# A two-layer diffusion backbone on one core: layer 1's modulation as row sums on the Vector Engine, and an opening with fewer, larger loads and idle transposes

## The chip, the cores and the metric

The kernel runs on one core of one Trainium2 chip. The metric is the device time of one execution in microseconds (us), the median over runs. Engines are named as in the profile: PE (TensorE matmuls), PEld (its weight loads), DVE (VectorE), ACT (ScalarE), POOL (GpSimd) and SP (SyncE, which issues most loads). Each of them takes its own instructions in a fixed order.

## The reference

512 latent tokens and 256 context tokens of width 1024 pass through two layers. Each layer is a mixer and a SwiGLU, and each of these is led by a norm that a modulation vector shifts and scales, and closed by a gate from the same vector:

```python
silu_c = jax.nn.silu(c)
silu_cc = jax.nn.silu(c_ctx)
for layer in range(DEPTH):
    need_ctx = layer < DEPTH - 1
    mod = (silu_c @ w_mod[layer] + b_mod[layer])[:, None, :]
    modc = silu_cc @ w_mod[layer] + b_mod[layer]
    sh1, sc1, g1, sh2, sc2, g2 = jnp.split(mod, 6, axis=-1)
    csh1, csc1, cg1, csh2, csc2, cg2 = jnp.split(modc, 6, axis=-1)
    h = modulate(rms_norm(x, norm_mix[layer]), sh1, sc1)
    hc = modulate(rms_norm(ctx, norm_mix[layer]), csh1, csc1)
    ...
    x = x + g1 * y
    x = x + g2 * swiglu(modulate(rms_norm(x, norm_ffn[layer]), sh2, sc2), w_ffn_in[layer], w_ffn_out[layer])
    if need_ctx:
        ctx = ctx + cg1 * yc
        ...
return rms_norm(x, norm_out)
```

The modulation of a layer is thus a product of one vector of 1024 (`silu(c)`) with a matrix of 1024 x 6144, and of a second vector (`silu(c_ctx)`) with the same matrix. In layer 1 the context is used only through `csh1` and `csc1`, the first third; its gates and its SwiGLU are not needed. Layer 0's mixer is global and windowed attention; layer 1's is neighbourhood attention and an RWKV-7 scan in two directions, which the kernel does in chunks with a small inverse.

## The kernel before, in words

All is fp32. A big product is done as three matmuls of rounded numbers: a weight tile of 128x1024 is loaded (`fetch`, L133), ACT rounds it into a high part `whi` (L143), and the rest, the low part `wlo`, is a subtraction (L145) on DVE, or on POOL while the flag `lo_pool` is set. Activations are split alike (`hxh`, `hxl`), and `mm3` (L387 to L389) issues high by high, high by low and low by high. `early` makes such a weight ahead of its use, and `onto`, `ffn` and `proj_in` consume them. Two buffers of each part exist, so PE works on one weight while the next is made.

The program is one stream of Python generators: a main line (for example the SwiGLU of layer 0 for x) calls `step(rate)`, which moves side work (`aside`, `beside`) on by so many yields. A scheduling layer turns that into one order per engine. In the stage that matters here, the main line is layer 0's output projection and SwiGLU for x, and beside it run the chain of layer 1's context (`ctx_chain`, with the RWKV inputs, the inverse `rwkv_inverse`, L1255 to L1267, and the scan) and, at half its rate (`M0`), the last two thirds of layer 1's modulation, `mods(1, 1)` and `mods(1, 2)`.

`mods` (L198 to L245) handles 2048 outputs. For each group of them it loads weights on a queue (POOL's here; 16 loads of 512 KB for each third, two buffers) and issues 32 matmuls (L224) with `silu_c`, a 128x32 operand of which two columns are used, into one of four column strips of a PSUM tile (`ps_m` here). In layer 1's last two thirds a matmul has 256 columns, and each third is two such groups of 32 matmuls; elsewhere it has 128 columns, and a third is four groups. (The profile counts two records for each.) Then ACT copies the result (L234), PE transposes it (L238), and DVE adds the bias and writes `mod` (L242). What uses these values is the gate of layer 1's mixer and layer 1's SwiGLU, well after the stage, and the norm that leads layer 1 reads the first third, which `mods(1, 0)` has made earlier.

The opening is `start` (L736 on) with `even_in` (L446 on). SP loads x in eight pieces, two tables, the weights of layer 0's first third of the modulation in pieces of 512 KB into eight slots, and after every fourth one a weight of the input projection; after the first four, the context in four pieces. ACT squares x (L309), DVE adds the squares (L311), PE sums them over partitions (L319), DVE makes the reciprocal root (L106 to L113), PE spreads it (L339); PE does the modulation (L224, L238); DVE and ACT then make the normed activations (`norm_k`, L378 to L380: a product on DVE, the shift and rounding on ACT, the low part on DVE), and PE begins the first input block (L465 to L467). `start` yields between these pieces. In the whole opening `lo_pool` is set, so the low parts of the first weights are made on POOL.

Of the kernel before, what the change touches and what calls it, by code (L numbers as in the profile page):

```python
# [20 lines left out]
KD = 8  # L21
# [14 lines left out]

S0, S1, S2, S3 = 6, 8, 4, 6
# [32 lines left out]
class Net:  # L70
# [93 lines left out]
    def setup(self):  # L164
        nc, ctx = self.nc, self.ctx
        self.cp = self.pool(ctx, "consts")
        self.cc = self.const("cc", [P, KD, 2])
        self.ident = self.t(self.cp, [P, P], "ident")
        make_identity(nc, self.ident)
        self.ones = self.t(self.cp, [P, 1], "ones")  # L170
        nc.vector.memset(self.ones, 1.0)
        self.zero1 = self.t(self.cp, [P, 1], "zero1")
        nc.vector.memset(self.zero1, 0.0)
        self.sc = self.t(self.cp, [P, KD, 32], "silu_c")
        nc.vector.memset(self.sc, 0.0)
# [21 lines left out]
    def mods(self, l, g, tmp, raws, dma, tag="t", hold=False):  # L197
# [49 lines left out]
        yield  # L247

# [195 lines left out]
    def even_in(self, tmp, hx, hc, kst, vt, start, rest):  # L444
# [3 lines left out]
        for blk in range(3):  # L448
            accs = [self.bank() for _ in range(TTILES)]
            for kp in range(4):  # L450
                if kp == blk == 0:
                    next(start)
                wh, wl = self.weight(self.ins["w0in"][blk, kp], 1024)
# [284 lines left out]
    def start(self, tmp, raws, hs):  # L738
# [3 lines left out]
        (X, _), (C, _) = self.streams  # L742
        for k in range(KD):
            nc.sync.dma_start(X[:, k, :], self.ins["xt"][:, k, :])
        self.bmod, self.nrm = self.const("bmod", [P, 2, 48]), self.const("nrm", [P, 5, 8])
        n = 0

        def dma(dst, src):
            nonlocal n
            nc.sync.dma_start(dst, src)  # L750
            n += 1
            if n % 4 == 0:
                self.fetch(self.ins["w0in"][0, n // 4 - 1])
            if n == 4:
                for k in range(0, KD, 2):
                    nc.sync.dma_start(C[:, k : k + 2, :], self.ins["ct"][:, k : k + 2, :])
# [20 lines left out]
        self.lo_pool = True  # L777
        self.early(None)
# [3 lines left out]
        self.norm_gain(0, 0, slice(0, None, 4))  # L782
        norms(0, 0)
        for q in range(4):
            for i in range(12):
# [15 lines left out]
    def layer0(self):  # L801
        nc, V = self.nc, self.nc.vector
        with ExitStack() as c1:
# [8 lines left out]
            with ExitStack() as c2:  # L812
# [8 lines left out]
                start = self.start(tmp, [r[:, 2 * i : 2 * i + 2, :] for r in raws for i in range(4)], {0: hx, 1: hc})  # L821
# [85 lines left out]
            with ExitStack() as c2:  # L907
# [3 lines left out]
                with ExitStack() as c3:  # L911
                    np_ = self.pool(c3, "nm1", 2)
                    raws = [self.t(wm, [P, 1, 1024], "wmod", bufs=2) for _ in range(2)]
                    rest = itertools.chain(*[self.mods(1, g, wm, raws, nc.gpsimd.dma_start, "m", True) for g in (1, 2)])
# [768 lines left out]
    def run(self):  # L1683
        self.setup()
        self.load_x()
        self.dr = self.pool(self.ctx, "dram", 1, bass.MemoryType.DRAM)
        self.biasd = self.t(self.dr, [P, 8, 4, 256], "biasd")
        self.layer0()
        self.layer1()


def prep(inputs):
# [9 lines left out]
    d["cc"] = c_(np.stack([g["c"][0], g["c_ctx"]], 1).reshape(KD, P, 2).transpose(1, 0, 2))  # L1702
    for l in range(2):
        for h in range(3):
            n = P if (l, h) < (1, 1) else 2 * P
            w = g["w_mod"][l][:, 2048 * h : 2048 * h + 2048].reshape(KD, P, 4, 512 // n, n).transpose(3, 1, 0, 2, 4)
            d[f"wmod{l}{h}"] = c_(w.reshape(512 // n, P, KD, 4 * n))
    d["bmod"] = c_(g["b_mod"].reshape(2, 48, P).transpose(2, 0, 1))
    nr = np.stack([g["norm_mix"][0], g["norm_ffn"][0], g["norm_mix"][1], g["norm_ffn"][1], g["norm_out"]])
    d["nrm"] = c_(nr.reshape(5, KD, P).transpose(2, 0, 1))  # L1710
# [80 lines left out]
```

## Time and profile before

| | |
|---|---|
| median of 3 runs | 2091.7 us (2090.3 to 2098.65) |
| the profiled execution | 2095.34 us, span 2093.4 us |
| mean granted TensorE clock | 0.967 |
| PE busy | 1981.8 us, 95% of the span |
| DVE busy | 1229.4 us, 59% |
| ACT busy | 893.1 us, 43% |
| POOL busy | 247.4 us, 12% |
| HBM traffic | 129 GB/s over the span |

A group's row of the profile reads: line, engine, operation, output<-inputs by the program's names, tile shape, count, busy time, mean ns of one, then the idle time of the engine just before and what ended it. A timeline's row starts with the start and the length of a run of equal instructions. In a table of stretches the granted clock (1.00 is full speed) stands behind the engines. Lines are those of the kernel before.

### The profile page before, as it was taken

The page shows a single profiled execution, that of the slowest core. Times are in us where ns is not written, and L with a number is a line of the kernel's source. Part 1 is how long each engine was busy: PE and PEld are TensorE (multiplying, and loading weights), DVE is VectorE, ACT ScalarE, POOL GpSimd, SP SyncE. Part 2 cuts the span into 40 slices and gives each one's busy share as a digit, 9 for nine tenths or more (in the row PEclk, how much of TensorE's full clock was granted, in tenths as well). Part 3 has the DMA queues.
Part 4 walks back from the last instruction along what each step waited for, and adds up shares of the span by engine and source line. Part 5 has one row for each costly group of instructions (what it writes and reads, how often), then busy time and mean ns, then how long its engine had stood idle before and what let it go on. Part 6 is the DMA issues. An engine that isn't in the chain of part 4 may idle for free.

```text
span 2093.4 us, 38293 instructions
## 1 busy us (share of the span) xinstructions
PE 1981.8 (95%) x15556; PEld 1611.0 (77%) x15556; DVE 1229.4 (59%) x2407; ACT 893.1 (43%) x1682; POOL 247.4 (12%) x366
## 2 busy tenths in 40 slices
PE   6999999999988999999999999889899989999997
PEld 4766778999986888787777776667667768888887
DVE  5756676666666443559445655775766774333335
ACT  3335557775733433552222355535345443222222
POOL 1111100000000010000112132322322120000000
PEclk9999999999999999999999998988889999999999
DMA  7353322444484445433434323455675133232321
GB/s 272 124 200 122 142 91 81 142 126 127 135 271 160 151 156 151 140 108 107 146 102 132 111 71 92 123 158 161 162 222 144 33 121 101 92 101 91 101 92 49
DMA packets 112655, 272.66 MB, mean 130 GB/s; under 512 B 15424, under 2 KB 48736, under 8 KB 110944
## 3 DMA queue, kind: packets, MB, share of 16 engines
q1 hardware_dynamic: 100256, 224.74, 34.4%
q0 software_dynamic: 12224, 45.49, 6.6%
q8 instruction: 122, 2.00, 0.4%
q14 instruction: 53, 0.43, 0.1%
HBM read 238.20 MB, written 31.98 MB: 129 GB/s over the span
## 4 chain that ended last, share of the span: by engine, by line
PE 74%; DVE 11%; issue 9%; DMA 2%; ACT 2%; POOL 1%; SPq 0%; DVEq 0%; POOLq 0%; ACTq 0%
PE ps_b L387 16%; PE ps_b L389 16%; PE ps_b L388 16%; PE ps_v L637 4%; PE ps_a L587 2%; PE ps_e L609 2%; PE ps_w L1311 2%; PE ps_w L1317 2%; PE ps_s L1340 1%; DVE kb L1262 1%; PE ps_w L1330 1%; DVE kb L1255 1%; DVE pi L1259 1%; PE ps_a L1047 1%; PE ps_e L1218 1%
## 5 line engine op out<-in xcount | busy, mean ns | idle before, releaser
L143 ACT CAST whi<-wraw 128x1024 fp32r<-128x1024 f32 (+2 forms) x291 | 292.7, 1008 | 669.8 <-PE ps_b L388 509.4
L145 DVE TENSOR_TENSOR wlo<-wraw,whi 128x1024 fp32r<-128x1024 f32 (+2 forms) x251 | 296.1, 1180 | 213.5 <-ACT whi L143 207.5
L387 PE MATMUL ps_b<-hxh,whi 128*128 128x512 f32 (+1 forms) x1040 | 402.4, 390 | 13.0 <-ACT cj L978 7.2
L388 PE MATMUL ps_b<-hxl,whi 128*128 128x512 f32 (+1 forms) x1040 | 397.8, 385 | 1.6 <-DVE hxl L380 1.5
L389 PE MATMUL ps_b<-hxh,wlo 128*128 128x512 f32 (+1 forms) x1040 | 397.3, 384 | 0.3 <-DVE wlo L145 0.2
L387 PEld LDWEIGHTS ps_b<-hxh,whi 128*128 128x128 f32 x1040 | 198.6, 192 | 60.6 <-ACT cj L978 7.8
L388 PEld LDWEIGHTS ps_b<-hxl,whi 128*128 128x128 f32 x1040 | 199.0, 192 | 40.1 <-DVE hxl L380 3.0
L389 PEld LDWEIGHTS ps_b<-hxh,wlo 128*128 128x128 f32 x1040 | 198.7, 192 | 39.6 <-DVE wlo L145 1.3
L387 PE MATMUL ps_b<-act,whi 128*128 128x512 f32 (+1 forms) x570 | 200.5, 352 | 4.6 <-ACT whi L143 2.8
L389 PE MATMUL ps_b<-act,wlo 128*128 128x512 f32 (+1 forms) x570 | 197.0, 346 | 1.5 <-DVE wlo L145 1.5
L388 PE MATMUL ps_b<-act,whi 128*128 128x512 f32 (+1 forms) x570 | 196.7, 345 | 0.6 <-DVE act L124 0.6
L387 PE MATMUL ps_b<-hch,whi 128*128 128x256 f32 x552 | 159.6, 289 | 0.1
L389 PE MATMUL ps_b<-hch,wlo 128*128 128x256 f32 x552 | 156.2, 284 | 0.4 <-DVE wlo L145 0.4
L388 PE MATMUL ps_b<-hcl,whi 128*128 128x256 f32 x552 | 155.9, 283 | 0.0
L387 PEld LDWEIGHTS ps_b<-act,whi 128*128 128x128 f32 x570 | 109.5, 192 | 22.7 <-issue 5.5
L389 PEld LDWEIGHTS ps_b<-act,wlo 128*128 128x128 f32 x570 | 109.6, 192 | 15.0 <-DVE wlo L145 2.1
L388 PEld LDWEIGHTS ps_b<-act,whi 128*128 128x128 f32 x570 | 109.6, 192 | 12.9 <-DVE act L124 1.0
L420 DVE SCALAR_TENSOR_TENSOR xx<-ps_b,mod,xx 128x512 f32<-128x512 f32 (+1 forms) x64 | 43.7, 684 | 120.6 <-PE ps_b L389 119.3
L145 POOL TENSOR_TENSOR wlo<-wraw,whi 128x1024 fp32r<-128x1024 f32 (+1 forms) x40 | 88.5, 2217 | 204.6 <-ACT whi L143 180.0
L713 DVE TENSOR_TENSOR ff_a<-ff_a,ps_b 128x512 f32<-128x512 f32 x44 | 30.2, 687 | 134.3 <-PE ps_b L389 133.6
L387 PEld LDWEIGHTS ps_b<-hch,whi 128*128 128x128 f32 x552 | 104.7, 190 | 5.7 <-issue 2.5
L389 PEld LDWEIGHTS ps_b<-hch,wlo 128*128 128x128 f32 x552 | 104.4, 190 | 1.7 <-DVE wlo L145 1.4
(373 smaller groups left out, 3470.6 us busy)
## 6 DMA issues: line engine op xcount, KB each, us to landing
wraw<-in_ffi SPq DMA_DIRECT2D x132, 512.0 KB, 3.5
xx<-in_wmod POOLq DMA_DIRECT2D x48, 512.0 KB, 5.0
wraw<-in_w1in SPq DMA_DIRECT2D x43, 512.0 KB, 3.6
wraw<-in_ffo SPq DMA_DIRECT2D x48, 448.0 KB, 3.3
wmod<-in_wmod POOLq DMA_DIRECT2D x32, 512.0 KB, 4.8
wraw<-in_ffo SPq DMA_DIRECT2D x24, 512.0 KB, 3.5
op<-op SPq DMA_DIRECT2D x32, 384.0 KB, 4.2
qx<-in_wmod SPq DMA_DIRECT2D x16, 512.0 KB, 6.7
```

The costliest lines, as they stand in the source:

```text
L143: self.nc.scalar.copy(hi[:, 0:n], raw)
L145: e.tensor_tensor(lo[:, 0:n], raw, hi[:, 0:n].bitcast(F32), op=ALU.subtract)
L387: mm(out, lhsT=wh, rhs=hh, start=first, stop=False)
L388: mm(out, lhsT=wh, rhs=hl, start=False, stop=False)
L389: mm(out, lhsT=wl, rhs=hh, start=False, stop=last)
L420: self.nc.vector.scalar_tensor_tensor(X[:, m, c], ps[:, 0:n][:, c], gate[:, m, i : i + 1], X[:, m, c], op0=ALU.mult, op1=ALU.add)
L587: nc.tensor.matmul(o, lhsT=q, rhs=k[:, b : b + o.shape[1]], start=i == 0, stop=i == len(passes) - 1)
L609: nc.tensor.transpose(pt[:, P * (j - c) : P * (j - c) + P], p[:, P * j : P * j + P], self.ident)
L637: self.nc.tensor.matmul(ps[HD * u : HD * u + HD, col : col + P], lhsT=vs[u][j], rhs=pts[u][:, j, :], start=j == 0, stop=j == nk - 1, tile_ ...
L713: V.tensor_tensor(a, a, pg[1][:, 0:w], op=ALU.mult)
L1311: mm(wy[HD * u + HD - W_ + r : HD * u + HD, p, :], lhsT=G[top[u], p, r:W_], rhs=VU[top[u], p, u, :], start=p == 0, stop=False, skip_group_ ...
L1317: mm(o, lhsT=AR[:, p, :], rhs=Sd[:, p, u, :], start=False, stop=not lat, skip_group_check=True)
```

## The change

There are four edits. First, the last two thirds of layer 1's modulation are made another way. The matrix is given transposed, so that 128 outputs lie on 128 partitions and the 1024 inputs along the row. The vector silu(c) is spread over all partitions by eight transposes and two ACT copies, and each of 32 tiles of 128 outputs is one DVE instruction, `tensor_tensor_reduce`, which multiplies the row by the vector, sums it and starts from the bias. Each is kept in its program order against all of DVE's other work. There are still 32 loads of 512 KB on POOL's queue, in three buffers; the next load is issued after each reduction. The second vector's values for these two thirds, which nothing uses, are set to zero. The 128 matmuls, their transposes, copies and bias additions are gone.

Second, the opening's loads: x as two pieces of 1 MB at the head of SP's queue, one table instead of three, the modulation's weights in pieces of 1 MB into four slots, a projection weight after every second, and the context as one piece after the third.

Third, 60 transposes of the identity into a PSUM bank that is overwritten later, issued in the program at the first input block.

Fourth, the first `early` comes after `norm_gain`, and `lo_pool` is set only after the first round, so that two low parts are made on DVE instead of POOL.

```diff
+    def mod_rows(self, l, tiles, tmp, dma, tag):
+        nc, V = self.nc, self.nc.vector
+        s = self.t(tmp, [P, 1024], "silu_r", bufs=1)
+        for h in range(2):
+            ps = self.bank(tag)
+            for j in range(4):
+                self.spread(ps[:, P * j : P * j + P], self.sc[:, 4 * h + j, 0:1].broadcast_to([P, P]))
+            nc.scalar.copy(s[:, 512 * h : 512 * h + 512], ps)
+        V.memset(self.mod[l][:, tiles[0] : tiles[-1] + 1, 1], 0.0)
+        todo, ahead = iter(tiles), []
+        def load():
+            t = next(todo, None)
+            if t is not None:
+                ahead.append(self.t(tmp, [P, 1024], "wmod", bufs=3))
+                dma(ahead[-1], self.ins[f"wmodT{l}"][t - tiles[0]])
+        load(), load(), load()
+        yield
+        for t in tiles:
+            w = ahead.pop(0)
+            self.tc.keep_in_program_order(
+                V.tensor_tensor_reduce(w, w, s, 1.0, self.bmod[:, l, t : t + 1], ALU.mult, ALU.add, self.mod[l][:, t, 0:1])
+            )
+            load()
+            yield
...
                 if kp == blk == 0:
                     next(start)
+                    for _ in range(WARM):
+                        nc.tensor.transpose(accs[0][:, 0:P], self.ident, self.ident)
...
-        for k in range(KD):
-            nc.sync.dma_start(X[:, k, :], self.ins["xt"][:, k, :])
-        self.bmod, self.nrm = self.const("bmod", [P, 2, 48]), self.const("nrm", [P, 5, 8])
...
-            if n % 4 == 0:
-                self.fetch(self.ins["w0in"][0, n // 4 - 1])
-            if n == 4:
-                for k in range(0, KD, 2):
-                    nc.sync.dma_start(C[:, k : k + 2, :], self.ins["ct"][:, k : k + 2, :])
+            if n % 2 == 0:
+                self.fetch(self.ins["w0in"][0, n // 2 - 1])
+            if n == 3:
+                nc.sync.dma_start(C, self.ins["ct"])
...
-        self.lo_pool = True
-        self.early(None)
...
         self.norm_gain(0, 0, slice(0, None, 4))
+        self.early(None)
         norms(0, 0)
         for q in range(4):
+            self.lo_pool = q > 0
...
-                    raws = [self.t(wm, [P, 1, 1024], "wmod", bufs=2) for _ in range(2)]
-                    rest = itertools.chain(*[self.mods(1, g, wm, raws, nc.gpsimd.dma_start, "m", True) for g in (1, 2)])
+                    rest = self.mod_rows(1, range(16, 48), wm, nc.gpsimd.dma_start, "m")
```

The order of the engines shows where this lands. The lines of the changed kernel are some 7 to 36 higher than those of the one before (the modulation's matmul L224 is L231 there, its transpose L238 is L245, the input block's L465 to L467 are L503 to L505, the spread L339 is L375, `mm3` L387 to L389 is L423 to L425, the low part L145 is L146, the inverse's L1259 and L1262 are L1292 and L1295).

First, PE at the start of the program, before; `qx` holds modulation weights, `hxh` and `hxl` the normed activations, `ps_t` and `ps_b` are PSUM tiles:

```order
L319 MATMUL ps_t_200<-ones_65,qc_136 128x1 x4
L224 MATMUL ps_t_219<-qx_45_130,silu_c_69 32x128 x8
L339 MATMUL ps_t_263<-ident_60,rms0y_206 128x128 x3
L224 MATMUL ps_t_219<-qx_45_130,silu_c_69 32x128 x8
L339 MATMUL ps_t_263<-ident_60,rms0y_206 128x128
L224 MATMUL ps_t_219<-qx_45_130,silu_c_69 32x128 x16
L238 MATMUL ps_t_269<-ident_60,qc_136 128x128
L465 MATMUL ps_b_179<-whi_259,hxh_11_85 128x512
```

And the same place in the changed kernel, where L490 is the idle transpose:

```order
L490 MATMUL ps_b_162<-ident_67 128x128 x29
L355 MATMUL ps_t_183<-ones_72,qc_138 128x1 x4
L231 MATMUL ps_t_202<-qx_45_132,silu_c_76 32x128 x16
L490 MATMUL ps_b_162<-ident_67 128x128 x8
L375 MATMUL ps_t_240<-ident_67,rms0y_189 128x128 x4
L231 MATMUL ps_t_202<-qx_45_132,silu_c_76 32x128 x16
L490 MATMUL ps_b_162<-ident_67 128x128 x4
L245 MATMUL ps_t_246<-ident_67,qc_138 128x128
L490 MATMUL ps_b_162<-ident_67 128x128 x19
L503 MATMUL ps_b_162<-whi_251,hxh_11_87 128x512
```

The 60 transposes stand in four places: ahead of everything, after the first half of the modulation's matmuls, before the transpose of their result, and before the first matmul of the input block.

Second, PE where layer 0's SwiGLU is led by its norm, before; `ps_m` is the modulation of layer 1, `rms0y` and `rms1y` are reciprocal roots:

```order
L339 MATMUL ps_b_7689<-ident_60,rms1y_7124 128x128 x2
L224 MATMUL ps_m_8140<-wmod_7245,silu_c_69 32x256 x4
L224 MATMUL ps_m_8140<-wmod_7246,silu_c_69 32x256 x4
L339 MATMUL ps_e_7756<-ident_60,rms0y_7610 128x128 x2
L319 MATMUL ps_e_7759<-ones_65,sq_a_1553_7273 128x1 x2
L224 MATMUL ps_m_8140<-wmod_7245,silu_c_69 32x256 x4
L224 MATMUL ps_m_8140<-wmod_7246,silu_c_69 32x256 x4
L387 MATMUL ps_b_7754<-hxh_1643_7726,whi_7744 128x256
```

And in the changed kernel:

```order
L375 MATMUL ps_b_7726<-ident_67,rms1y_7163 128x128 x2
L375 MATMUL ps_m_8031<-ident_67,silu_c_76 128x128 x4
L375 MATMUL ps_e_7793<-ident_67,rms0y_7647 128x128 x2
L355 MATMUL ps_e_7796<-ones_72,sq_a_1549_7310 128x1 x2
L375 MATMUL ps_m_8037<-ident_67,silu_c_76 128x128 x4
L423 MATMUL ps_b_7791<-hxh_1639_7763,whi_7781 128x256
```

Where the first sixteen modulation matmuls stood among the norm's spreads, the eight transposes of silu(c) stand now.

Third, DVE inside the inverse of layer 1's context (its steps are L1259 and L1262; `wlo` is the low part of a weight), before:

```order
L145 TENSOR_TENSOR wlo_10273<-wraw_10270,whi_10272 128x1024
L1259 TENSOR_TENSOR pi_10251<-kb_10249,kb_10250 128x87
L1262 TENSOR_TENSOR kb_10250<-kb_10250,pi_10251 128x29x3
L1259 TENSOR_TENSOR pi_10251<-kb_10249,kb_10250 128x112
L1262 TENSOR_TENSOR kb_10250<-kb_10250,pi_10251 128x28x4
L1259 TENSOR_TENSOR pi_10251<-kb_10249,kb_10250 128x135
```

And in the changed kernel, where L280 is the reduction and, as a row of its own, the read of its accumulator:

```order
L146 TENSOR_TENSOR wlo_10324<-wraw_10321,whi_10323 128x1024
L125 TENSOR_TENSOR act_10265<-ff_a_2066_10263,act_10264 128x512
L1292 TENSOR_TENSOR pi_10272<-kb_10270,kb_10271 128x156
L1295 TENSOR_TENSOR kb_10271<-kb_10271,pi_10272 128x26x6
L280 ISA wmod_9985,mod_9_80<-wmod_9985,silu_r_8030,c_tab_65 128x1024
L280 ISA mod_9_80 128x1
L1292 TENSOR_TENSOR pi_10272<-kb_10270,kb_10271 128x175
L1295 TENSOR_TENSOR kb_10271<-kb_10271,pi_10272 128x25x7
```

Eight of the 32 reductions stand between the first and the last step of that inverse; 15 stand ahead of it and nine behind it.

More of the change, by code (lines that the diff above doesn't have):

```diff
@@ L35 @@
 NKB = 2
+WARM = 60
 S0, S1, S2, S3 = 6, 8, 4, 6
@@ L165, in setup @@
         nc, ctx = self.nc, self.ctx
+        self.load_x()
+        X = self.streams[0][0]
+        for k in range(0, KD, 4):
+            nc.sync.dma_start(X[:, k : k + 4, :], self.ins["xt"][:, k : k + 4, :])
         self.cp = self.pool(ctx, "consts")
-        self.cc = self.const("cc", [P, KD, 2])
+        tab = self.const("tab", [P, 152])
+        self.cc = tab[:, 0:16].rearrange("p (k s) -> p k s", s=2)
+        self.bmod, self.nrm = (tab[:, a:b].rearrange("p (l j) -> p l j", l=l) for a, b, l in ((16, 112, 2), (112, 152, 5)))
         self.ident = self.t(self.cp, [P, P], "ident")
@@ L741, in start @@
         nc = self.nc
-        (X, _), (C, _) = self.streams
-        for k in range(KD):
-            nc.sync.dma_start(X[:, k, :], self.ins["xt"][:, k, :])
-        self.bmod, self.nrm = self.const("bmod", [P, 2, 48]), self.const("nrm", [P, 5, 8])
+        C = self.streams[1][0]
         n = 0
@@ L820, in layer0 @@
                 tmp = Slots(self.t(ap_, [P, 16 * NCTX], "qc"), 2)
-                start = self.start(tmp, [r[:, 2 * i : 2 * i + 2, :] for r in raws for i in range(4)], {0: hx, 1: hc})
+                start = self.start(tmp, [r[:, 4 * i : 4 * i + 4, :] for r in raws for i in range(2)], {0: hx, 1: hc})
                 next(start)
@@ L1684, in run @@
         self.setup()
-        self.load_x()
         self.dr = self.pool(self.ctx, "dram", 1, bass.MemoryType.DRAM)
@@ L1701, in prep @@
     d["ct"] = c_(g["ctx"][0].T.reshape(KD, P, NCTX).transpose(1, 0, 2))
-    d["cc"] = c_(np.stack([g["c"][0], g["c_ctx"]], 1).reshape(KD, P, 2).transpose(1, 0, 2))
+    cc = np.stack([g["c"][0], g["c_ctx"]], 1).reshape(KD, P, 2).transpose(1, 0, 2)
     for l in range(2):
         for h in range(3):
[L1705 to L1708, printed above, removed]
+            if (l, h) < (1, 1):
+                w = g["w_mod"][l][:, 2048 * h : 2048 * h + 2048].reshape(KD, P, 4, 4, P).transpose(3, 1, 0, 2, 4)
+                d[f"wmod{l}{h}"] = c_(w.reshape(4, P, KD, 4 * P))
+    d["wmodT1"] = c_(g["w_mod"][1][:, 2048:].T.reshape(32, P, KD * P))
+    bmod = g["b_mod"].reshape(2, 48, P).transpose(2, 0, 1)
     nr = np.stack([g["norm_mix"][0], g["norm_ffn"][0], g["norm_mix"][1], g["norm_ffn"][1], g["norm_out"]])
-    d["nrm"] = c_(nr.reshape(5, KD, P).transpose(2, 0, 1))
+    nr = nr.reshape(5, KD, P).transpose(2, 0, 1)
+    d["tab"] = c_(np.concatenate([x.reshape(P, -1) for x in (cc, bmod, nr)], 1))
     w = g["w_in_even"][0]
```

## The prediction

> **What bounds the kernel now.** I read the page first: the shares of the engines and the chain that ended last.
>
> ```profile
> span 2093.4 us, 38293 instructions
> PE 1981.8 (95%) x15556; PEld 1611.0 (77%) x15556; DVE 1229.4 (59%) x2407; ACT 893.1 (43%) x1682; POOL 247.4 (12%) x366
> PE 74%; DVE 11%; issue 9%; DMA 2%; ACT 2%; POOL 1%; SPq 0%; DVEq 0%; POOLq 0%; ACTq 0%
> ```
>
> TensorE is busy for 95% of the span and is 74% of the chain. So an instruction taken from PE is worth its own time, but only in stages where PE is what ends last; DVE holds 11% of the chain, so there are stages where work given to DVE costs as much. The stages decide. The next view is the table of stretches over all engines, from the end of layer 0's mixer to layer 1's opening, where all of the removed matmuls stand. Columns: stretch, its length, then busy time (with instructions) of PE, PEld, DVE, ACT and POOL, granted clock, DMA share, GB/s.
>
> ```profile
> 650.00:665.00 15.00, 9.10 (x79) 6.21 (x77) 13.43 (x43) 7.26 (x15) 2.10 (x4) 0.80 0.59 187
> 665.00:690.00 25.00, 24.63 (x180) 18.95 (x181) 16.06 (x42) 10.88 (x22) 3.16 (x6) 0.91 0.49 157
> 690.00:930.00 240.00, 238.45 (x1478) 196.47 (x1477) 108.08 (x158) 107.87 (x177) 11.18 (x35) 1.00 0.46 140
> 930.00:1000.00 70.00, 67.24 (x340) 53.35 (x339) 59.20 (x97) 17.32 (x21) 0.00 (x0) 0.98 0.38 119
> 1000.00:1170.00 170.00, 170.00 (x1579) 128.29 (x1578) 79.02 (x125) 46.30 (x74) 28.88 (x49) 1.00 0.39 123
> 1170.00:1190.00 20.00, 16.41 (x149) 13.89 (x149) 11.88 (x29) 6.08 (x12) 4.82 (x4) 0.78 0.41 147
> 1190.00:1210.00 20.00, 16.73 (x116) 14.04 (x115) 16.72 (x46) 9.33 (x18) 3.62 (x4) 0.93 0.07 26
> ```
>
> In 665 to 930 and 1000 to 1170 PE has no room and DVE is under half busy, save at the start. In 650 to 665 and 930 to 1000 it is the other way: DVE 13.43 of 15 and 59.20 of 70.
>
> **What the removed matmuls cost.** The same stretches for the modulation's PSUM tile alone (its matmuls and transposes):
>
> ```profile
> 650.00:665.00 15.00, 3.23 (x32) 0.82 (x32) 0.00 (x0) 0.00 (x0) 0.80 0.59 187
> 665.00:690.00 25.00, 6.73 (x50) 1.75 (x50) 0.24 (x2) 0.37 (x1) 0.91 0.49 157
> 690.00:930.00 240.00, 7.12 (x76) 2.44 (x76) 0.24 (x2) 0.38 (x1) 1.00 0.46 140
> 930.00:1000.00 70.00, 0.00 (x0) 0.00 (x0) 0.00 (x0) 0.00 (x0) 0.98 0.38 119
> 1000.00:1170.00 170.00, 8.77 (x88) 2.75 (x88) 0.31 (x2) 0.37 (x1) 1.00 0.39 123
> 1170.00:1190.00 20.00, 2.22 (x17) 0.78 (x17) 0.00 (x0) 0.37 (x1) 0.78 0.41 147
> sum 560.00, PE 28.67 PEld 8.72 DVE 1.01 ACT 1.49; mean PE 4.10 PEld 1.25 DVE 0.14 ACT 0.21
> PE ps_m L224 <- DMA wmod<-in_wmod: 6.0, 4, 2.7
> ```
>
> So 28.67 us of PE go. The last row is from the waits of PE in 600 to 1200: four times PE, which takes its queue in order, stood 6.0 us in all before a modulation matmul whose weights had not landed. In 650 to 665 that and the 3.23 us are mostly cover for the norms on DVE (13.43 of 15), so I count 0.8 us there. In 665 to 690 PE is full and the 6.73 us count: together 7.5. In 690 to 930 the 7.12 count, in 1000 to 1170 the 8.77. The rest (28.67 less the rows above, 2.8 us) lies in 1170 to 1210, where PE idles 6.9 us in 40 and the norms of layer 1 set part of the pace: I count 2.0. Sum: 7.5 + 7.1 + 8.8 + 2.0 = 25.4 us gained. Added to PE there: eight transposes that spread silu(c), about 1 us with their place in the queue. The 32 loads stay on the POOL queue with their size; the four ACT copies become two.
>
> **What the reductions cost.** 32 of them go to DVE, each over 128x1024 with two SBUF operands and a read of the accumulator. The trace shows no such one. The nearest rows: a custom DVE operation of 512 columns with its accumulator read, and ordinary subtractions of 512 and 1024 columns from two SBUF operands.
>
> ```profile
> L598 DVE CUSTOM_DVE_ANT_0 sm_p<-ps_a,zero,sm_m 128x512 f32<-128x512 f32 x32 | 23.9, 746 | 4.3 <-PE ps_a L587 3.9 <-ACT sm_p L599 0.2
> L598 DVE DVE_READ_ACCUMULATOR2_ANT sm_m<- 128x1 f32 x64 | 5.3, 83 | 0.0
> L145 DVE TENSOR_TENSOR wlo<-wraw,whi 128x512 fp32r<-128x512 f32 x8 | 5.5, 683 | 0.0
> L145 DVE TENSOR_TENSOR wlo<-wraw,whi 128x1024 fp32r<-128x1024 f32 x195 | 238.4, 1223 | 189.1 <-ACT whi L143 183.6
> ```
>
> 512 more columns cost 1223 - 683 = 540 ns, so a reduction is estimated at 746 + 540 + 83 = 1.37 us, 32 of them 44 us. The upper bound is two passes of 746 for each half and twice that rate: 2 x 746 x 2 less overheads, some 2.5 us. I take 1.37, because the 1223 ns row already has two SBUF operands and falls on the line of its smaller form.
>
> [...]
>
> Where do they lie? DVE takes its queue in order and each reduction is held at its place in the program, so what stands behind one is late by its length: most often the next low part of a weight (L145), and behind that PE. By the order, eight reductions stand inside the decoding of layer 1's inverse, the one place where DVE has no room:
>
> ```profile
> 935.71 8.37 DVE L1255 STREAM_TRANSPOSE kb<-G 32x1024 f32<-32x1024 f32 x4 [0.23 <-PE ps_e L1220]
> 935.00:950.00 15.00, 15.00 (x69) 12.29 (x69) 14.14 (x23) 3.37 (x4) 0.00 (x0) 1.00 0.37 106
> 950.00:965.00 15.00, 14.75 (x65) 11.50 (x64) 14.42 (x30) 5.25 (x7) 0.00 (x0) 1.00 0.26 73
> 965.00:980.00 15.00, 13.20 (x50) 10.11 (x49) 14.21 (x32) 2.50 (x3) 0.00 (x0) 0.89 0.26 85
> ```
>
> No modulation matmul stood there, so PE gains nothing, and 8 x 1.37 = 11 us of DVE are added to a stretch in which DVE idles 2.2 us in 45. The low parts between the steps of the inverse feed PE, so PE waits about what is left: 9 us lost (between 3, if the two weights that are ready ahead absorb it, and 18, at 2.4 us each). Outside, a low part waits on ACT's cast before it for 183.6 us in all, so a reduction mostly falls into that wait; with a few where the weight's matmuls are short, I take 1.5 us lost (0 to 5).
>
> **The opening.** PE's timeline and two neighbours of it, before:
>
> ```profile
> 12.17 1.87 PE L319 MATMUL ps_t<-ones,qc 128*128 128x1 f32 x8 [12.17 <-DVE qc L311]
> 18.58 1.94 PE L224 MATMUL ps_t<-qx,silu_c 128*32 128x128 f32 x32
> 20.91 0.33 PE L238 MATMUL ps_t<-ident,qc 128*128 128x128 f32 x1 [0.39 <-ACT qc L234]
> 23.32 0.73 PE L465 MATMUL ps_b<-whi,hxh 128*128 128x512 f32 x2 [2.08 <-ACT hxh L379]
> 24.78 1.22 PE L466 MATMUL ps_b<-wlo,hxh 128*128 128x512 f32 x2 [0.73 <-POOL wlo L145]
> 31.39 0.39 PE L467 MATMUL ps_b<-whi,hxl 128*128 128x512 f32 x1
> 35.23 1.95 PE L224 MATMUL ps_t<-qx,silu_c 128*32 128x128 f32 x64
> 42.28 0.50 PE L465 MATMUL ps_b<-whi,hxh 128*128 128x512 f32 x1 [2.00 <-ACT hxh L379]
> 24.00:31.00 7.00, 6.27 (x15) 4.45 (x15) 5.57 (x10) 3.72 (x9) 0.73 (x1) 0.51 1.04 405
> 38.55 2.38 POOL L145 TENSOR_TENSOR wlo<-wraw,whi 128x1024 fp32r<-128x1024 f32 x1 [13.82 <-ACT whi L143]
> 38.63 2.84 DVE L378 SCALAR_TENSOR_TENSOR qc<-xx,an,qc 128x512 f32<-128x512 f32 x1
> L378 DVE SCALAR_TENSOR_TENSOR qc<-xx,an,qc x8: 739/750/2899, 21.8 to 63.1; 128x512 f32<-128x512 f32 x8
> ```
>
> Three things can be won. First, a cold PE: 32 records take 1.94 us at 18.58 and 64 take 1.95 at 35.23, and in 24 to 31 the granted clock is 0.51. In 7 us that is 3.4 us of matmul time, and about 2 us more on the way to 23.32. The 60 idle transposes are to keep PE running ahead of it; 19 of them stand between L238 and the first L465, where PE waits 2.08 us. Second, the low part on POOL: L466 waits for it 0.73 us, and the norm on DVE at 38.63 takes 2.84 us beside it where its shortest is 0.739; so the wait of 2.00 us at 42.28 should go with the second low part moved to DVE, at the price of 1.2 us twice on DVE. Third, fewer and larger loads: the first square can start only when 1 MB of x has landed instead of 256 KB, the last one is about as early, so I count half a microsecond lost there and half gained by the shorter queue of issues. These overlap, since DVE is itself busy 5.57 of 7 us in 24 to 31: of 3.4 + 2 + 2 = 7.4 us I take 4.5 (0 to 7.4).
>
> [...]
>
> **The sum.** Against the profiled execution's 2095.3 us (its span is 2093.4): -4.5 (opening) - 25.4 (matmuls) + 1 (spread) + 9 (inverse) + 1.5 (late low parts) = -18.4 us, hence 2076.9 for such an execution. The median of the runs, 2091.7, lies 3.6 below this execution; I apply the same difference to it: 2073. About 0.5%, 10.5 us, is what a measurement here can tell from no change; faster thus means below 2081.3.
>
> **The rivals.**
> Forecast, all terms about as above: 2073, chance 0.50.
> Full gain: the weights ready ahead cover the reductions in the inverse (3 us instead of 9, nothing elsewhere) and the opening gives 7. That is 2073 - 6 - 1.5 - 2.5 = 2063. For it: at 935.71 DVE spends 8.37 us on transposes and PE stays at 15.00 of 15. Against: PE falls to 13.20 of 15 by 965. Chance 0.15.
> [...] Chance 0.12.
> [...] Chance 0.16.
> Slower: the reductions wait for their loads. Each load is issued by POOL only after the reduction that frees its buffer, and POOL's queue also holds steps of layer 1's scan over the context (28.88 us busy in 1000 to 1170); a load behind such a step is late, the reduction held in its place waits for it, and DVE, the low parts behind it and PE with them. By the order nine reductions stand in that stage. At 3.2 us late each on PE it is 29 us: 2073 + 29 = 2102, the point from which the change loses by 0.5%. For it: PE stood 6.0 us before such loads already. Against: three buffers instead of two, and 170 us for nine reductions, some 19 us from one to the next. Chance 0.07.
>
> **How the numbers follow.** Faster: forecast, full gain and no warming, 0.77, less 0.02 for the far end of the inverse's price: 0.75. Same: half rate and that far end, 0.18. Slower: 0.07. The range leaves out the slow case and a part beyond the full gain: from 2058 (the full gain and the parts of 25.4 that I did not count, 3.3 us, and 2 us on the low parts' path) to 2088 (half rate, with 3.5 us less won in the opening).
>
> **What would show it.** Right: the stretch after 650 shows no modulation matmul, each reduction takes 1.3 to 1.5 us, PE is still full in the stretches of 690 to 930 and 1000 to 1170, which are shorter by 7 and 9 us, PE's idle time in the inverse grows by about 9, and layer 0's second weight starts near 38 instead of 42.28. Wrong: reductions above 2 us; waits of DVE's reductions for their loads; a granted clock of half after the first input matmul; or PE's idle time in the inverse unchanged, which would put the gain near 2063.

## The result, and the profile after

The changed kernel takes 2080.55 us (median of 5 runs, 2078.02 to 2084.48), the one before 2096.36 us beside it (5 runs, 2090.3 to 2098.65). The ratio is 0.9935, with a 95% interval from 0.9913 to 0.9957: 13.6 us faster by that ratio (15.8 by the two medians), where the sum gave 18.4. The change profiled at 2083.11 us, 12.2 less than the execution before. In what follows two executions are left out because they fell in a slow state: 2214.03 us in double_rows, which is the profiled one, so that kernel has no profile to compare by stages, and 8934.53 us in double_others. The page after, at its head:

```profile
span 2081.3 us, 37907 instructions
PE 1970.1 (95%) x15360; PEld 1615.4 (78%) x15360; DVE 1263.2 (61%) x2466; ACT 893.9 (43%) x1681; POOL 246.9 (12%) x364
PE 74%; DVE 12%; issue 6%; DMA 3%; ACT 2%; POOL 1%; SPq 0%; DVEq 0%; ACTq 0%; POOLq 0%
```

PE is busy 11.7 us less, and DVE 33.8 us more. The total lies within 5 us of the sum on record. Its parts do not agree. To see that, the same matmul (the n-th of its line and tile) was looked up in both traces, and the table gives its start after, less its start before. Between two columns stands what that stretch won.

| start in the kernel before | 42.3 | 179.6 | 645 | 690 | 930 | 1005 | 1165 | 1205 | 1700 |
|---|---|---|---|---|---|---|---|---|---|
| the change | -1.5 | -1.0 | -0.5 | -5.6 | -4.6 | -6.3 | -12.0 | -14.1 | -12.9 |

From 645 to 1205 the change wins 13.6 us; by the sum it should have been 13.9 (25.4 less 1, 9 and 1.5). But in 690 to 930, where 7.1 were counted, it lost 1.0, and from 930 to 1205, where 8.8 and 2.0 less the 9 of the inverse make 1.8, it won 9.5. Two errors of some 8 us cancelled.

A part of the 9.5 us is, by estimate, clock and not work. The granted clock is 0.89 in 965 to 980 of before, a row that the prediction shows, and 0.87 in the first row here, also of before; the two rows below it are of the change, over the same work:

```profile
1165.00:1205.00 40.00, 35.17 (x334) 30.37 (x333) 30.16 (x77) 14.12 (x29) 6.66 (x7) 0.87 0.27 93
```

```profile
959.00:974.00 15.00, 13.66 (x59) 10.72 (x59) 14.55 (x30) 3.11 (x5) 1.06 (x2) 1.00 0.54 163
1153.00:1191.00 38.00, 33.84 (x316) 29.83 (x315) 30.34 (x76) 13.76 (x28) 7.25 (x7) 0.91 0.28 98
```

If PE's work takes longer by what the clock withholds, that is 0.11 x 15 + 0.13 x 40 - 0.09 x 38 = 3.4 us, an estimate. It leaves some 6 us of the 9.5, nearly all of it from 1005 to 1165, where the clock is 1.00 in both and the change wins 5.6. Whether the change brought the better clock is not shown.

The table of stretches after, over the same work as the stretches shown of before from 665 on, so a few us earlier:

```profile
662.00:685.00 23.00, 20.90 (x131) 19.17 (x132) 18.95 (x50) 12.88 (x25) 0.13 (x2) 0.85 0.14 44
685.00:925.00 240.00, 231.65 (x1397) 193.49 (x1396) 124.07 (x183) 106.65 (x175) 14.89 (x38) 1.00 0.48 148
925.00:993.00 68.00, 66.44 (x345) 53.10 (x344) 63.52 (x112) 17.36 (x21) 4.75 (x9) 1.00 0.53 162
993.00:1161.00 168.00, 167.34 (x1513) 128.49 (x1512) 97.39 (x148) 46.25 (x74) 28.86 (x44) 1.00 0.39 123
```

In the 240 us of the second row PE now idles 8.35 us; before it was 1.55. So the matmuls there were replaced by nothing. In the third row, the inverse, PE idles 1.56 us, less than the 2.76 of before, though DVE is busy 63.52 of 68. The reduction itself is as estimated. This is its group on the page's list:

```profile
L280 DVE CUSTOM_DVE_ANT_0 wmod<-wmod,silu_r,c_tab 128x1024 f32<-128x1024 f32 x32 | 41.5, 1298 | 0.3
```

1.30 us and 0.08 for the accumulator's read (82 ns, the median of the 32), against 1.37 taken. Reductions above 2 us, a sign of being wrong on record, are not seen: the longest took 1.74.

### The profile page after: what moved, and what is told of

The parts are those of the page before. It is cut to its first block, busy times and chain, and to the rows that moved or that the text cites. A ratio compares the mean times of both kernels' runs of the same rounds, so it can differ in the third digit from the quotient of the medians.

```text
span 2081.3 us, 37907 instructions
## 1 busy us (share of the span) xinstructions
PE 1970.1 (95%) x15360; PEld 1615.4 (78%) x15360; DVE 1263.2 (61%) x2466; ACT 893.9 (43%) x1681; POOL 246.9 (12%) x364
## 4 chain that ended last, share of the span: by engine, by line
PE 74%; DVE 12%; issue 6%; DMA 3%; ACT 2%; POOL 1%; SPq 0%; DVEq 0%; ACTq 0%; POOLq 0%
PE ps_b L423 17%; PE ps_b L424 16%; PE ps_b L425 16%; PE ps_v L675 4%; PE ps_a L625 2%; PE ps_e L647 2%; PE ps_w L1344 1%; PE ps_w L1350 1%; DVE kb L1295 1%; PE ps_s L1373 1%; PE ps_w L1363 1%; DVE pi L1292 1%; PE ps_e L1251 1%; PE ps_a L1080 1%; DVE kb L1288 1%
## 5 line engine op out<-in xcount | busy, mean ns | idle before, releaser
L423 PE MATMUL ps_b<-hxh,whi 128*128 128x512 f32 (+1 forms) x1040 | 405.4, 393 | 17.0 <-ACT cj L1011 7.2
L146 DVE TENSOR_TENSOR wlo<-wraw,whi 128x1024 fp32r<-128x1024 f32 (+2 forms) x253 | 299.0, 1182 | 201.6 <-ACT whi L144 195.6
L425 PE MATMUL ps_b<-hxh,wlo 128*128 128x512 f32 (+1 forms) x1040 | 399.7, 386 | 0.0
L423 PEld LDWEIGHTS ps_b<-hxh,whi 128*128 128x128 f32 x1040 | 201.0, 194 | 61.2 <-ACT cj L1011 7.8
L425 PEld LDWEIGHTS ps_b<-hxh,wlo 128*128 128x128 f32 x1040 | 201.2, 194 | 39.5 <-DVE wlo L146 1.1
L423 PE MATMUL ps_b<-act,whi 128*128 128x512 f32 (+1 forms) x570 | 198.6, 348 | 7.3 <-ACT whi L144 4.1
L425 PE MATMUL ps_b<-act,wlo 128*128 128x512 f32 (+1 forms) x570 | 196.8, 345 | 1.4 <-DVE wlo L146 1.4
L423 PE MATMUL ps_b<-hch,whi 128*128 128x256 f32 x552 | 159.3, 289 | 4.2 <-ACT cj L975 2.1
L425 PE MATMUL ps_b<-hch,wlo 128*128 128x256 f32 x552 | 155.9, 283 | 0.7 <-DVE wlo L146 0.7
L423 PEld LDWEIGHTS ps_b<-act,whi 128*128 128x128 f32 x570 | 108.8, 191 | 22.4 <-ACT whi L144 4.3
L425 PEld LDWEIGHTS ps_b<-act,wlo 128*128 128x128 f32 x570 | 108.7, 191 | 15.4 <-DVE wlo L146 2.6
L424 PEld LDWEIGHTS ps_b<-act,whi 128*128 128x128 f32 x570 | 108.8, 191 | 13.3 <-DVE act L125 0.8
L423 PEld LDWEIGHTS ps_b<-hch,whi 128*128 128x128 f32 x552 | 104.1, 189 | 8.7 <-ACT cj L975 2.6
L146 POOL TENSOR_TENSOR wlo<-wraw,whi 128x1024 fp32r<-128x1024 f32 (+1 forms) x38 | 83.9, 2214 | 205.9 <-ACT whi L144 181.4
L425 PEld LDWEIGHTS ps_b<-hch,wlo 128*128 128x128 f32 x552 | 104.2, 189 | 1.7 <-DVE wlo L146 1.4
L424 PEld LDWEIGHTS ps_b<-hcl,whi 128*128 128x128 f32 x552 | 104.6, 190 | 0.9 <-issue 0.2
```

What stands on the lines that cost most here:

```text
L146: e.tensor_tensor(lo[:, 0:n], raw, hi[:, 0:n].bitcast(F32), op=ALU.subtract)
L423: mm(out, lhsT=wh, rhs=hh, start=first, stop=False)
L424: mm(out, lhsT=wh, rhs=hl, start=False, stop=False)
L425: mm(out, lhsT=wl, rhs=hh, start=False, stop=last)
```

## What the matmuls in 690 to 930 had been worth

One place shows it. This is PE's timeline of before, at the end of a projection of the context:

```profile
795.24 0.38 PE L996 MATMUL ps_b<-ident,cj 128*128 128x128 f32 x2
795.55 0.64 PE L224 MATMUL ps_m<-wmod,silu_c 128*32 128x256 f32 x8
796.73 0.50 PE L387 MATMUL ps_b<-hxh,whi 128*128 128x512 f32 x1 [0.54 <-ACT cj L942]
```

And the same place after (there L1029 is what L996 is before, and L975 is L942):

```profile
789.57 0.38 PE L1029 MATMUL ps_b<-ident,cj 128*128 128x128 f32 x2
790.64 0.36 ACT L975 COPY cj<-ps_b 128x256 f32<-128x256 f32 x1
791.06 0.50 PE L423 MATMUL ps_b<-hxh,whi 128*128 128x512 f32 x1 [1.11 <-ACT cj L975]
```

From the transposes to the next projection it is 1.49 us before and 1.49 after. Before, four modulation matmuls filled a part of it and PE waited 0.54 us; after, PE waits 1.11. It waits for ACT, which copies a projection out of a PSUM bank (`ps_b`): there are two of these banks, and the next projection needs one. It is not the only such place. PE's waits for these copies in 690 to 930 of before, and then over the same work (685 to 925) after, as total, times and longest:

```profile
PE ps_b L387 <- ACT cj L942: 0.5, 1, 0.5
```

```profile
PE ps_b L423 <- ACT cj L975: 3.2, 3, 1.1
PE ps_b L423 <- ACT cj L1140: 0.9, 1, 0.9
```

They grow from 0.5 to 4.1 us, about half of PE's 8.35 us of idle time. So the row of 238.45 busy in 240 was right, but part of that busy time was cover. The theory from here on, the cover theory: matmuls that stood in such hand-overs were worth nothing, and the reductions cost PE nothing as long as the low parts of the weights keep their pace. The rival is the bookkeeping of the prediction: a matmul is worth its time, and the reductions cost 10.5 us of it on PE.

## The experiments

Ratios are to the kernel before, with 95% intervals; between two of the changed kernels a difference under some 5 us is not clear by the times alone. The stretches are read from one profile each, in the way of the table above.

**rows_only**: the row sums alone.

```diff
 (the kernel before)
+    def mod_rows(self, l, tiles, tmp, dma, tag):
...
+                    rest = self.mod_rows(1, range(16, 48), wm, nc.gpsimd.dma_start, "m")
```

> The kernel before with the modulation's row sums alone; the opening is that of before. Both theories agree in the sign. Cover theory (part of the removed matmuls stood in waits of PE, the reductions cost PE nothing): 9 to 12 us faster than before, some 2085, with PE's opening as before (first input matmul near 23.3, second weight near 42.3) and PE idle 8 to 9 us in the 120 us after 740, against 1.6 before. Bookkeeping theory of the prediction (matmuls worth 25.4, reductions cost 10.5, spread 1): 14 us faster, 2082, with PE's added idle time in the inverse instead.

Measured: 2081.59 us, 0.9945 (0.9927 to 0.9963). It wins 4.9 us in 645 to 690, 0.4 in 690 to 930 and 9.3 in 930 to 1205, the pattern of the change. PE idles 7.3 us in the 120 us after 744 (1.55 before). The ratio makes 11.5 us, inside the 9 to 12 of the cover theory; the 14 of the bookkeeping is not excluded by its interval. So the gain is that of the row sums, and where it lies does not come from the opening.

**open_only**: the new opening, with the modulation by matmuls.

```diff
 (the changed kernel)
-                    rest = self.mod_rows(1, range(16, 48), wm, nc.gpsimd.dma_start, "m")
+                    rest = itertools.chain(*[self.mods(1, g, wm, raws, nc.gpsimd.dma_start, "m", True) for g in (1, 2)])
```

> The new opening (loads, idle transposes, two low parts on DVE) with the modulation by matmuls as before. From the profile of the change: second weight at 40.8 instead of 42.3, PE 3.3 us ahead at 55 to 120 us, of which 2.4 are left at 560: 2 to 4 us faster than before, some 2093. By the prediction's term: 4.5 us faster, 2092. If the row sums had been all of the gain: no change.

Measured: 2093.55 us, 1.0007 (0.9993 to 1.0021). The second weight starts at 41.0 instead of 42.3, and PE is 1.0 us ahead at 179.6 and 0.7 at 645; in the time of the whole program no gain is measured. Both expectations of a gain were too high.

**short_rows** and **double_rows**: the reductions made short (8 columns of 1024, which leaves out nearly all of the sum), and done twice.

```diff
 (short_rows)
-                V.tensor_tensor_reduce(w, w, s, 1.0, self.bmod[:, l, t : t + 1], ALU.mult, ALU.add, self.mod[l][:, t, 0:1])
+                V.tensor_tensor_reduce(w[:, 0:8], w[:, 0:8], s[:, 0:8], 1.0, self.bmod[:, l, t : t + 1], ALU.mult, ALU.add, self.mod[l][:, t, 0:1])
 (double_rows)
+            for o in (self.mod[l][:, t, 0:1], s2):
```

> The change with each reduction over 8 columns instead of 1024 (leaves out nearly all of the sum; loads, buffers and order stay). Cover theory: the reductions delay the inverse on DVE but nothing that PE waits for, so the time is within 2 us of the change, 2079 to 2082. Bookkeeping theory: the 10.5 us that the reductions cost PE come back, 2070; of them 9 in the inverse.

> The change with each reduction done twice (the second one's result is not used). Cover theory: the inverse on DVE is another 11 us later and PE still does not wait for it: 0 to 3 us slower than the change, 2081 to 2084. Bookkeeping theory: 32 more reductions cost PE once more what the first cost, 9 to 13 us: 2090 to 2094.

Measured: short_rows 2080.15 us, 0.9936 (0.9920 to 0.9952), the same as the change; in 645 to 1205 it wins 15.4 us where the change wins 13.6. So by the stage 32 reductions of 1.3 us cost some 2 us, and by the times less than the 10.5 of the bookkeeping. That speaks for cover. double_rows takes 2094.09 us, 0.9997 (0.9980 to 1.0014): 13 us slower than the change, what the bookkeeping gave. Neither theory has both. The first 44 us on DVE are nearly free and the next 44 are not: there is a slack, and the question became where it runs out.

**double_inverse** and **double_others**: only the eight reductions inside the inverse doubled, or only the other 24.

```diff
 (double_inverse)
-            for o in (self.mod[l][:, t, 0:1], s2):
+            for o in (self.mod[l][:, t, 0:1], s2)[: 2 if 15 <= t - tiles[0] < 23 else 1]:
 (double_others)
+            for o in (self.mod[l][:, t, 0:1], s2)[: 1 if 15 <= t - tiles[0] < 23 else 2]:
```

> The change with only the eight reductions inside the inverse doubled: 11 us more of DVE there. Theory that the inverse has a slack on PE's side which the single reductions used up: most of the 14 us that doubling all cost comes from here, 8 to 12 us slower than the change, about 2090, with PE idle where the scan waits for the inverse. Rival, that the cost of doubling lies where low parts of weights come late: 0 to 3 us slower, 2081 to 2084.

> The change with only the other 24 reductions doubled. Slack theory: 0 to 4 us slower than the change, 2081 to 2085. Rival (late low parts): 10 to 14 us slower, 2091 to 2094.

Measured: double_inverse 2080.72 us, 0.9938 (0.9918 to 0.9958); double_others 2085.64 us, 0.9964 (0.9949 to 0.9979). By the medians the inverse can take twice the reductions at no cost and the others cost 5.1 us. The first is what the rival expected and not the slack theory, the second lies just above what the slack theory expected; neither theory has both.

The profiles show more, of one execution each. In double_others PE loses 6.7 us in 690 to 930 (from -7.4 to -0.7 in the terms of the table), where the change loses 1.0. Late low parts are not among PE's waits there, and PE idles 9.8 us against 8.35. By estimate the larger part is clock:

```profile
855.00:869.00 14.00, 12.43 (x69) 9.42 (x68) 10.59 (x19) 5.76 (x11) 0.53 (x1) 0.76 0.67 199
```

In the change the clock is 1.00 in 855 to 865, over about the same work. 0.24 x 14 makes 3.4 us, an estimate. (The order of PE's instructions differs a little at that place too.)

In double_inverse PE loses 8.1 us against the change from 930 to 1205, nearly all at one place. PE's longest wait in 950 to 1015 there, DVE's rows at its end, and the ten us from it on:

```profile
PE ps_b L425 <- DVE xx L458: 4.8, 1, 4.8
1004.10 5.90 DVE L1302 STREAM_TRANSPOSE G<-kb 32x1024 f32<-32x1024 f32 x3
1010.03 0.75 DVE L458 SCALAR_TENSOR_TENSOR xx<-ps_b,mod,xx 128x512 f32<-128x512 f32 x1
1010.00:1020.00 10.00, 9.07 (x53) 6.70 (x53) 3.02 (x3) 0.00 (x0) 0.00 (x0) 0.66 0.79 244
```

The residual sum (L458), which reads a bank of the projections, stands behind three of the inverse's closing transposes in DVE's order. PE waits 4.8 us for it, and behind the wait the granted clock is 0.66 for 10 us, where the change has 1.00 over the same work: another 3.4 us by estimate. So a slack that ends with the inverse's end is seen in this profile. But that execution then took 13.3 us less than the change from 1205 to 1700 (more on this stretch below), and the medians show no cost, so it is not shown that every execution pays it. What doubling all costs, 13 us, is more than its two parts; that stays open.

**fill_early** and **fill_late**: 64 matmuls of the removed form back beside the first 16 or the last eight reductions.

```diff
+            if t < tiles[0] + 16:
+                for i in range(4):
+                    nc.tensor.matmul(
+                        fil[32 * (i % 4) : 32 * (i % 4) + 32, 0:256], lhsT=self.sc[:, i % 8, :],
+                        rhs=w[:, 256 * (i % 4) : 256 * (i % 4) + 256], start=True, stop=True, tile_position=(0, 32 * (i % 4)),
+                    )
 (fill_late: t >= tiles[0] + 24, and range(8))
```

> The change with 64 matmuls of the removed form (128x32 by 256 columns, on the weights just loaded, result not used) put back beside its first 16 reductions, that is ahead of the inverse: twelve at the norm that leads layer 0's SwiGLU, 52 between 690 and 980. Such a matmul took 0.22 us busy in the kernel before. Cover theory: they run in PE's waits for ACT and cost little, 0 to 4 us beside the change: 2081 to 2085. Bookkeeping theory: 64 x 0.22 = 14 us: 2094.

> The same 64 matmuls put back beside the last eight reductions, behind the inverse, in a stretch where PE is full in the change as it was before. Both theories: 10 to 14 us slower than the change, 2091 to 2094. If it were no more than fill_early, the cover theory would have the wrong place.

Measured: both 2087.15 us, 0.9957 (0.9943 to 0.9971) and 0.9959 (0.9945 to 0.9972). The medians don't tell the two places apart: both are some 5 us slower than the change by the ratios, more than was expected of the early matmuls and less than of the late ones. By the condition on record with fill_late that speaks against the place that the cover theory names. The profiles, one execution each, do tell them apart. The stretches of their PSUM tile, of fill_early and then of fill_late:

```profile
690.00:930.00 240.00, 7.43 (x88) 1.96 (x88) 0.00 (x0) 1.00 0.48 147
```

```profile
1010.00:1210.00 200.00, 11.36 (x128) 4.48 (x128) 0.00 (x0) 0.97 0.33 106
```

Against the change, fill_early loses 1.5 us from 645 to 930, with 44 matmuls of 7.43 us busy in 690 to 930 and 12 more ahead of it. fill_late loses 9.0 us from 930 to 1165, with 64 matmuls of 11.36. So a matmul in the first place is nearly free and in the second is worth four fifths of its time. fill_early loses 3.6 us more from 930 to 1005, beside its last eight matmuls in the inverse: the granted clock is 0.72 in 998 to 1004, which makes 1.7 us by estimate, and PE idles 1.8 us more than in the change. Why it does is not shown.

**third_bank**: the bank that held the modulation's results is free after the change. It goes to the projections.

```diff
-                self.psum(self.cK, True, b=2, m=1)
+                self.psum(self.cK, True, b=3)
-                    rest = self.mod_rows(1, range(16, 48), wm, nc.gpsimd.dma_start, "m")
+                    rest = self.mod_rows(1, range(16, 48), wm, nc.gpsimd.dma_start, "b")
```

> The change with the PSUM bank that held the removed matmuls' results given to the projections, three banks instead of two. In the change PE waits 1.1 us each time the next projection needs a bank that ACT is still copying out. If these hand-overs are what the removed matmuls had covered, PE's idle time in the 120 us after 744 falls from 8.3 to 3 us or less and the kernel is 4 to 6 us faster than the change, 2075. If PE waits there for the values themselves, and not for the bank, the same time as the change.

Measured: 2071.6 us, 0.9892 (0.9873 to 0.9912), 9 us faster than the change. The stretches of the four 30-us rows in which the change has 26.64, 28.89, 27.76 and 28.38 busy:

```profile
744.00:774.00 30.00, 30.00 (x211) 26.11 (x211) 17.97 (x35) 11.71 (x21) 3.42 (x8) 1.00 0.43 128
774.00:804.00 30.00, 30.00 (x169) 26.29 (x168) 12.69 (x14) 10.53 (x16) 4.09 (x8) 1.00 0.57 175
804.00:834.00 30.00, 30.00 (x169) 25.75 (x168) 13.90 (x16) 10.05 (x16) 1.06 (x2) 1.00 0.59 189
834.00:864.00 30.00, 29.66 (x213) 22.21 (x213) 23.25 (x40) 20.46 (x41) 2.11 (x4) 1.00 0.54 160
```

PE's idle time falls from 8.3 to 0.3 us, and from 690 to 930 it wins 7.4 us, just the 7.1 that the prediction had counted. The place that was shown above, at 789.57 in the change, is here:

```profile
787.16 0.38 PE L1029 MATMUL ps_b<-ident,cj 128*128 128x128 f32 x2
787.30 0.48 PE L423 MATMUL ps_b<-hxh,whi 128*128 128x512 f32 x1
```

From the transposes to the next projection it is 0.14 us, where it was 1.49. So the wait was for the bank and not for values, and the gain was to be had with it. With three banks some small steps of the context's chain also stand elsewhere in PE's order between 750 and 850; what they alone are worth was not tried.

**no_warm**, **lo_on_pool**, **loads_before**: one part of the opening undone at a time.

```diff
 (no_warm)
-WARM = 60
+WARM = 0
 (lo_on_pool)
-            self.lo_pool = q > 0
+        self.lo_pool = True
 (loads_before)
-            nc.sync.dma_start(X[:, k : k + 4, :], self.ins["xt"][:, k : k + 4, :])
+            nc.sync.dma_start(X[:, k, :], self.ins["xt"][:, k, :])
...
```

> The change without the idle transposes. If they keep PE's clock up: half clock after the first input matmul again, and the second weight and the 24th input matmul 2 to 3 us later than in the change (40.8 and 62.0 there). If PE-mode transposes do not count for the clock: no difference, or half a microsecond earlier.

> The change with the first two low parts on POOL again. If POOL's subtraction is what held up the norm on DVE beside it: a norm of about 2.8 us again, the second weight 1 to 2 us later than 40.8. Else the same.

> The change with the opening loads of before (idle transposes and low parts as in the change). First sum of squares near 12.2 instead of 13.5. If the larger loads help: second weight later than 40.8 by 1 us or more. If they only delay the first sum: second weight 1 us earlier, 39.8.

Rows of the opening on PE, of the change:

```profile
1.37 6.07 PE L490 MATMUL ps_b<-ident 128*128 128x128 f32 x29 [1.37 <-POOL ident masks.py:199]
13.54 1.86 PE L355 MATMUL ps_t<-ones,qc 128*128 128x1 f32 x8 [6.10 <-DVE qc L347]
17.19 1.97 PE L490 MATMUL ps_b<-ident 128*128 128x128 f32 x8
21.86 2.24 PE L490 MATMUL ps_b<-ident 128*128 128x128 f32 x19
24.82 0.40 PE L503 MATMUL ps_b<-whi,hxh 128*128 128x512 f32 x1
33.84 0.40 PE L375 MATMUL ps_t<-ident,rms1y 128*128 128x128 f32 x2 [2.31 <-DVE rms1y L114]
40.79 0.50 PE L503 MATMUL ps_b<-whi,hxh 128*128 128x512 f32 x1
```

And of no_warm:

```profile
24.40 0.80 PE L503 MATMUL ps_b<-whi,hxh 128*128 128x512 f32 x1 [3.14 <-ACT hxh L415]
25.42 0.63 PE L503 MATMUL ps_b<-whi,hxh 128*128 128x512 f32 x1
27.71 0.39 PE L505 MATMUL ps_b<-whi,hxl 128*128 128x512 f32 x1
34.15 0.67 PE L375 MATMUL ps_t<-ident,rms1y 128*128 128x128 f32 x2 [2.22 <-DVE rms1y L114]
41.09 0.50 PE L503 MATMUL ps_b<-whi,hxh 128*128 128x512 f32 x1
```

Without the transposes the first matmuls take 0.80 and 0.63 us and are down to 0.39 at 27.71; with them they take 0.40 from 24.82 on. The granted clock in 24 to 31 is 1.00 in both, so it is the times of the matmuls that show a difference here. In the change the clock is 0.50 in the seven us up to 20.55 and 1.00 behind them:

```profile
13.54:20.55 7.01, 7.01 (x64) 6.13 (x68) 1.80 (x11) 0.50 (x1) 0.00 (x0) 0.50 1.03 430
20.56:24.10 3.54, 3.54 (x53) 3.05 (x43) 1.90 (x4) 2.01 (x4) 0.00 (x0) 1.00 1.02 382
```

What transposes alone do is seen at the start of the change, where nothing else runs on PE. The first 29 of them as min, median and max in ns, up to 6.7 us and from there:

```profile
L490 PE MATMUL ps_b<-ident x25: 421/421/475, 1.4 to 6.5; 128*128 128x128 f32 x25
L490 PE MATMUL ps_b<-ident x4: 272/273/351, 6.8 to 7.2; 128*128 128x128 f32 x4
```

So with transposes alone on PE their median came down from 421 to 273 ns; the granted clock is 1.00 in 1.37 to 6.70 already. The eight at 17.19, at a clock of 0.50, take 421 again, and the 19 from 21.86 on, at 1.00, take 273. The first 29 are of no use to the matmuls, though: PE then stands idle for 6.10 us, and from 13.54 on the clock is 0.50. The last 19, which end at 24.10, run at 1.00 from their start. And the second weight is only 0.3 us earlier (40.79 against 41.09): in both, PE waits over 2 us for the second norm's reciprocal root at about 34, and what PE had saved goes into that wait. no_warm takes 2075.62 us, 0.9906 (0.9887 to 0.9924), not slower than the change; the two intervals overlap and no stage explains a gain, so whether the transposes cost anything stays open.

lo_on_pool takes 2080.42 us, 0.9931 (0.9913 to 0.9949). Its second weight starts at 42.77, 2.0 us later than the change's. The first pair of norms on DVE, and then POOL beside it:

```profile
22.32 3.52 DVE L414 SCALAR_TENSOR_TENSOR qc<-xx,an,qc 128x512 f32<-128x512 f32 x2
```

```profile
22.45 2.83 POOL L146 TENSOR_TENSOR wlo<-wraw,whi 128x1024 fp32r<-128x1024 f32 x1 [21.14 <-ACT whi L144]
```

Two norms take 3.52 us while POOL subtracts, as in the kernel before; in the change, with the low part on DVE, none of these norms takes more than 0.75. loads_before takes 2079.28 us, 0.9921 (0.9904 to 0.9938); its first sum is at 11.85 and its second weight at 40.41, 0.4 us earlier than the change's. So the larger loads won nothing on PE. Of the three edits the low parts on DVE are what moves the second weight, by 2.0 us; at the last input block (179.6 in the kernel before) lo_on_pool is within 0.2 us of the change, and that gain is gone too.

## Why the prediction was right in the sum and wrong in its parts

**The removed matmuls.** Counted: 7.5 us at the norm of the SwiGLU, 7.1 in 690 to 930, 8.8 in 1000 to 1170, 2.0 behind. Found at the same places: 5.1, a loss of 1.0, 5.6 (1005 to 1165) and 2.1 (1165 to 1205), and of the last some 1.8 are clock by the estimate above. The step that failed is "PE has no room, so the 7.12 count". A full row says that PE had something to issue all the time; whether that sets the pace is seen only where it is taken out, or in what PE waits for right behind it (ACT cj, 0.54 us at 796.73, was in the trace).

**The reductions.** Their price was right (1.38 us against 1.37). The 18 us at the far end of the inverse's price, and the 2088 of the range, take 2.4 us for a reduction; no run shows that, and what was measured is 1.30 us and 0.08 for the read, little more than the 1.22 us of the plain subtraction of that size. Their place was right too: DVE's chain of the inverse is longer. In the kernel before it goes from 935.71 to the first closing transpose at 976.62, 40.9 us; after:

```profile
932.16 8.36 DVE L1288 STREAM_TRANSPOSE kb<-G 32x1024 f32<-32x1024 f32 x4
986.61 2.07 DVE L1300 STREAM_TRANSPOSE G<-kb 32x1024 f32<-32x1024 f32 x1
```

54.5 us, 13.5 more. The step that failed is the next one, "PE waits about what is left: 9 us lost". From 930 to 1005 PE lost nothing: it won 1.8 us, about what the better clock there is worth (0.11 x 15 = 1.65 us by estimate). The inverse is side work: the SwiGLU's weights get their low parts between the reductions in good time (PE waits 0.4 us for them in 950 to 1015), and no wait of PE for the inverse's result is seen. The profile of double_inverse shows where that ends.

**The opening.** Counted 4.5 us, found 1.5 at the second weight, 0.5 at 645 and nothing in open_only's time. Of the three terms that make 7.4, the two of the cold PE (3.4 and 2 us) failed: PE's first matmuls are faster (0.40 us from 24.82 on against 0.63 in no_warm), but what they saved went into another wait, for the second norm's reciprocal root (2.31 us at 33.84), which the sum does not have. The half clock itself, 0.51 in 24 to 31 before, is 1.00 there in the change and in no_warm too. The third, the low part beside the norm, was right in size (2.0 against 2) and was lost again later. The loads were counted at nothing on balance and won nothing.

**Luck.** That the sum came out within 5 us of the time is luck: a gain that was not there and a loss that was not there cancelled, and some 3.4 us of the profiled gain are clock by estimate, which the sum does not have. Two of the signs on record say so: PE was not full in 690 to 930, and its idle time in the inverse did not grow, a sign of being wrong that was to put the time near 2063. It did not come to that because the matmuls were worth less.

**The rivals.** Slower needed reductions that wait for their loads: the 32 reductions waited 0.3 us in all. Of no warming and half rate, which the chances also count: the first matmuls of the change took 0.40 us from 24.82 on (0.63 in no_warm), and a reduction 1.30 us. The full gain was nearest the mechanism, in that the reductions cost PE next to nothing; it lacked the cover.

## What to carry to other kernels

Before counting an instruction's time as gain, look at what its engine waits for right behind it: work that stands in the hand-over of a buffer can be free, and then taking it away wins nothing until the hand-over goes too (here 1.0 us was lost in 690 to 930 without 7.12 us of matmuls, and 7.4 won once there was a third bank). When a removal frees a buffer, give it to the neighbour that waits; here that was worth 9 us, two thirds as much again as the change. And a sum that comes out right is no proof of its terms: compare the same instruction's start in both traces, stage by stage, with the granted clock beside it.

## What the runs showed that was not expected

From 1205 to 1700, where the instructions of all these kernels are the same but for the third bank, the profiled executions differ by far more than the 0.5% that the change is about: 494.9 us before, 496.1 in the change, 486.7 in rows_only, 482.8 in double_inverse. The granted clock differs with them; here this stretch of the change, and then of double_inverse:

```profile
1191.00:1687.00 496.00, 454.10 (x4652) 342.74 (x4651) 339.72 (x652) 232.11 (x465) 138.82 (x175) 0.91 0.45 130
```

```profile
1199.50:1682.35 482.85, 444.30 (x4653) 335.68 (x4652) 340.30 (x652) 232.17 (x465) 139.62 (x175) 0.94 0.47 134
```

0.03 of some 490 us is 15 us by estimate, and the two differ by 13.3, so the clock is enough to make the difference. What sets the clock was not tried. It means that one profile's end time cannot settle a few us here. The stage in which the edit lies can do better, but only with its granted clock beside it: from 1005 to 1165 no_warm, with the instructions of the change, wins 2.7 us where the change wins 5.6; its clock is 0.83 in 1003 to 1013, against 1.00 in the change, and its PE idles 1.3 us.
